# A two-layer decoder step on one core: where the memory block's residual comes from, where the last norm stands, and where staged operands lie

## The chip, the cores and the metric

The kernel runs on 1 core of a Trainium2 chip. The metric is device time in microseconds (us) of the whole program. Engines are named as in the profile: PE (TensorE), DVE (VectorE), ACT (ScalarE), POOL (GpSimd), SP (SyncE, which here only issues DMAs).

## The reference, cut to what matters

One inference step of two layers for a prompt (1 x 1024 tokens) and a sample group (8 x 8 tokens), together 1088 tokens of 1024 features, in float32. Each layer is a mixing block, then cross-attention into 256 memory tokens, then a convolutional feed-forward block:

```python
for l in range(DEPTH):
    ...                                   # l = 0: mix_ab, l = 1: sliding-window attention
    xp = xp + yp
    xs = xs + ys
    ...
    xp = xp + mem_attend(rmsnorm(xp, ln_mem[l]), mk, mv, m_w_q[l], m_q_gain[l], m_w_o[l])
    ...
    fp, cp = conv_ffn(rmsnorm(xp, ln_ffn[l]), zc, f_w_up[l], f_conv_w[l], f_conv_b[l], f_w_down[l])
    ...
    xp = xp + fp

def conv_ffn(h, g_ctx, w_up, conv_w, conv_b, w_down):
    up = h @ w_up
    g, u = up[..., :D_FF], up[..., D_FF:]
    ...                                   # gc = causal conv of g, 3 taps
    y = (gelu(gc) * u) @ w_down
```

## The kernel before

Activations are kept feature-major: 8 blocks of 128 features by tokens. Tokens come in three chunks `CHS` of 384, 384 and 320 (c = 0, 1, 2) for the attention blocks and in two halves of 544 (q = 0, 1) for the feed-forward block. Each float32 operand is split into a high part and a rest (ACT copies to float32r, DVE subtracts), and each product is three matmuls (`mm3`).

PE's order is the program's, written out by hand. The order on the other engines and DMA queues is made by a planner that simulates the program ahead of time; each engine and each queue then runs in order.

**State.** The SBUF tile `big` holds the split residual `xh`, `xl` of all chunks. In feed-forward the same bytes hold `B0`, the operands of half q = 0 in seven products (names 1, 5, 6, 2, 3, 7, 4, in steps of 8 QT with QT = 272 columns); the last 8 QT serve for raw loads (`hx_of`) and for parts to be stored (`part`).

**x_update (L309)** adds a block of output projection to the residual. In the mixing blocks it reads xh and xl, stores the sum to DRAM (`xd`, one tensor for each chunk) and splits it again. In mem() it loads the block from `xd` into a tile of the ring `tmp` (5 buffers), adds on DVE, and stores to `xq`, a DRAM tensor for each half. `squares` (L296) adds the squares into `acc[c]`: block 0 by ACT alone, odd blocks on POOL, even ones on DVE.

**Norms.** `norm_chunk(c)` (L343) takes column sums of `acc[c]` by matmul with ones (L336), then a power on POOL (L331); `factors(c)` (L733) calls `spread`, which puts the factors on a diagonal (DVE, L375), spreads them by matmul (L376) and copies them to `rvq` (L379).

**Output projection of mem()** (L957 on): six jobs (hf, c) in the order (0,0), (1,0), (0,1), (1,1), (0,2), (1,2), each with four blocks m of 12 matmuls. `next(parts)` steps through the attention of the samples in between. The norm of chunk 0 stands ahead of (1,1), that of chunk 1 ahead of (0,2), followed by `build()`, which makes B0; the norm of chunk 2 stands after (1,2).

**ffn() (L1112).** `up_operands` (L1073) loads a raw pair of blocks from `xq` by SP, scales it by gain and factor (L1080) and makes the seven operands (L1092 splits, L1097 differences). Half 1 (tile set `b`) is built before the jobs. Each job of `seven` (L998) is seven products of 12 matmuls; products 7 and 4 of a job run within the next one. `gate_out` and `up_out` empty PSUM; `up_out` stores the operands of the down projection to DRAM (`hd`).

**Down projection** (L1305 on): `load_b` (L1316) loads operands on POOL's queue: 1, 5, 6 come already split, straight into one of 15 rotating tiles (10 of them in `big`); 2, 3, 7, 4 come whole into `hx`, one of 4 pool tiles, and are split by ACT and DVE (L1326, L1327). `down_out` adds `xq` through a tile `xr`.

## Time and profile before

| | |
|---|---|
| Runs | 2695.42, 2697.85, 2699.47 us (median 2697.85) |
| Profiled execution | 2697.89 us, of which its span 2695.8 us |
| PE busy in the span | 93% |
| DVE, ACT, POOL busy | 73%, 45%, 18% |
| Mean granted clock of PE | 0.962 of 2.4 GHz |

A row of a timeline is one instruction or several merged ones: start, duration (for merged ones first to last), engine, line, operation, output and inputs with their shapes, count, and in brackets the time the engine was idle before it and what ended that. The windows give the busy time of each engine within a stretch.

### The profile page before, as it was taken

What the parts mean: (1) busy time and instruction counts of PE and PEld (TensorE: products, weight loads), DVE (VectorE), ACT (ScalarE), POOL (GpSimd) and SP (SyncE); (2) the same over time, 40 slices, a digit from 0 to 9 for tenths busy, and PEclk for the clock granted to TensorE, in tenths of its full rate; (3) what the DMA queues carried; (4) which work ended last, traced back from release to release, by engine and by line L of the source; (5) the groups of instructions that cost most, each with busy time, mean ns of one, the idle gap of its engine ahead of it and who ended that gap; (6) DMA issues with size and microseconds to landing.
All of it is one profiled execution on the core that took longest, in us unless ns stands there. A gap on an engine that the chain in (4) does not pass through costs nothing.

```text
span 2695.8 us, 46361 instructions
## 1 busy us (share of the span) xinstructions
PE 2510.7 (93%) x17136; PEld 2317.7 (86%) x17136; DVE 1962.6 (73%) x4514; ACT 1226.4 (45%) x2687; POOL 481.6 (18%) x440
## 2 busy tenths in 40 slices
PE   8999999769999998999899989998599999998998
PEld 6898987569999998999776767876499999998998
DVE  8646964588777786888657676853888778776885
ACT  5223644254545454433546554552454545544231
POOL 3506432110000001111533333421100000002100
PEclk9999999779999999999999998998799999999999
DMA  8302213534233336553211022215424233347642
GB/s 270 107 19 81 83 57 109 169 97 131 91 129 111 125 123 206 207 197 137 66 38 47 1 69 75 87 45 179 135 89 131 94 126 119 117 153 261 221 136 87
DMA packets 239714, 318.12 MB, mean 118 GB/s; under 512 B 18946, under 2 KB 199264, under 8 KB 239487
## 3 DMA queue, kind: packets, MB, share of 16 engines
q1 hardware_dynamic: 227454, 253.87, 29.4%
q0 software_dynamic: 12032, 61.28, 6.2%
q8 instruction: 135, 2.21, 0.3%
q14 instruction: 93, 0.75, 0.1%
HBM read 224.08 MB, written 90.93 MB: 117 GB/s over the span
## 4 chain that ended last, share of the span: by engine, by line
PE 68%; DVE 12%; issue 7%; DMA 5%; POOL 3%; ACT 2%; SPq 0%; POOLq 0%; DVEq 0%; ACTq 0%
PE psa L1007 8%; PE psa L1009 8%; PE psa L1008 8%; PE psb L1009 6%; PE psb L1007 6%; PE psb L1008 6%; PE psa L259 5%; PE psa L260 5%; PE psa L261 5%; DVE s L350 3%; PE psb L167 2%; DMA hx<-hd 1%; DMA t<-xd 1%; PE psb L842 1%; PE psb L817 1%
## 5 line engine op out<-in xcount | busy, mean ns | idle before, releaser
L1055 ACT ACTIVATE w<-st 128x512 fp32r<-128x512 f32 (+2 forms) x532 | 298.7, 572 | 382.7 <-PE psb L1009 115.3
L1056 DVE TENSOR_TENSOR w<-st,w 128x512 fp32r<-128x512 f32 (+2 forms) x532 | 327.4, 621 | 168.7 <-ACT w L1055 163.1
L1007 PE MATMUL psa<-big,w 128*128 128x272 f32 x1160 | 340.8, 294 | 11.0 <-DVE x L1343 7.3
L1009 PE MATMUL psa<-big,w 128*128 128x272 f32 x1160 | 338.7, 292 | 0.0
L1008 PE MATMUL psa<-big,w 128*128 128x272 f32 x1160 | 337.3, 291 | 0.0
L1007 PE MATMUL psb<-big,w 128*128 128x272 f32 x952 | 276.1, 290 | 19.1 <-ACT big L1326 19.1
L1007 PE MATMUL psa<-b,w 128*128 128x272 f32 x952 | 276.8, 291 | 12.4 <-ACT b L1091 7.0
L1008 PE MATMUL psa<-b,w 128*128 128x272 f32 x952 | 275.8, 290 | 4.4 <-DVE b L1092 4.4
L1009 PE MATMUL psa<-b,w 128*128 128x272 f32 x952 | 276.4, 290 | 0.0
L1009 PE MATMUL psb<-big,w 128*128 128x272 f32 x952 | 276.3, 290 | 0.0
L1008 PE MATMUL psb<-big,w 128*128 128x272 f32 x952 | 275.7, 290 | 0.5 <-DVE big L1327 0.5
L1007 PEld LDWEIGHTS psa<-big,w 128*128 128x128 f32 x1160 | 222.3, 192 | 14.9 <-DVE x L1343 8.7
L1008 PEld LDWEIGHTS psa<-big,w 128*128 128x128 f32 x1160 | 222.3, 192 | 0.0
L1009 PEld LDWEIGHTS psa<-big,w 128*128 128x128 f32 x1160 | 222.1, 191 | 0.0
L260 PE MATMUL psa<-s,w 128*128 128x384 f32 (+1 forms) x576 | 198.4, 344 | 17.9 <-DVE s L350 17.6
L259 PE MATMUL psa<-s,w 128*128 128x384 f32 (+1 forms) x576 | 198.1, 344 | 7.1 <-DVE t L319 3.6
L1322 POOL DMA_DIRECT2D big<-hd x36 | 21.7, 603 | 1022.1 <-PE psa L1009 988.4
L1007 PEld LDWEIGHTS psb<-big,w 128*128 128x128 f32 x952 | 180.9, 190 | 19.6 <-ACT big L1326 19.6
L261 PE MATMUL psa<-s,w 128*128 128x384 f32 (+1 forms) x576 | 194.0, 337 | 0.0
L1007 PEld LDWEIGHTS psa<-b,w 128*128 128x128 f32 x952 | 179.7, 189 | 14.0 <-ACT b L1091 7.4
L1008 PEld LDWEIGHTS psa<-b,w 128*128 128x128 f32 x952 | 180.6, 190 | 5.5 <-DVE b L1092 5.5
L1009 PE MATMUL psb<-b,w 128*128 128x272 f32 x632 | 183.5, 290 | 0.0
(352 smaller groups left out, 6765.6 us busy)
## 6 DMA issues: line engine op xcount, KB each, us to landing
st<-in_f_w_up_dram SPq DMA_DIRECT2D x88, 512.0 KB
hd<-big SPq DMA_DIRECT2D x264, 136.0 KB
hd<-m SPq DMA_DIRECT2D x176, 136.0 KB
hx<-hd POOLq DMA_DIRECT2D x48, 408.0 KB, 6.4
big<-hd POOLq DMA_DIRECT2D x24, 816.0 KB, 7.4
st<-in_f_w_down_dram SPq DMA_DIRECT2D x48, 384.0 KB
b<-hd POOLq DMA_DIRECT2D x12, 816.0 KB, 6.7
big<-xq SPq DMA_DIRECT2D x32, 272.0 KB
```

Source lines behind the costliest of these rows:

```text
L167: T.transpose(out, in_, idt[:rows, :rows])
L259: mm(out, lhsT=ah, rhs=bh, start=first, stop=False)
L260: mm(out, lhsT=ah, rhs=bl, start=False, stop=False)
L261: mm(out, lhsT=al, rhs=bh, start=False, stop=last)
L350: V.tensor_tensor(out=t[:, 1, :src_n], in0=src, in1=f(t[:, 0, :src_n]), op=ALU.subtract)
L817: mm(ps[:, j, :], lhsT=qt[:, 2 * hh + j, :], rhs=kt[:, 2 * hh + j, :], start=True, stop=True)
L842: mm(ps[:, :n], lhsT=vm[:, kb, 128 * h:128 * h + 128], rhs=pts[c][h][:, kb, :n], start=(kb == 0), stop=(kb == 1))
L1007: mm(ps[:, :QT], lhsT=wt[:, 0, k, :], rhs=bt[:, 0, k, :], start=first and k == 0, stop=False, skip_group_check=True)
L1008: mm(ps[:, :QT], lhsT=wt[:, 0, k, :], rhs=bt[:, 1, k, :], start=False, stop=False, skip_group_check=True)
L1009: mm(ps[:, :QT], lhsT=wt[:, 1, k, :], rhs=bt[:, 0, k, :], start=False, stop=k == nk_of(j) - 1, skip_group_check=True)
L1055: S.activation(t[:, 0], src, AF.Copy)
L1056: V.tensor_tensor(out=t[:, 1], in0=src, in1=f(t[:, 0]), op=ALU.subtract)
```

## The change

For chunks 0 and 1 the residual in mem() is added from xh and xl in SBUF; for chunk 2 it is loaded from DRAM, for all eight blocks ahead of the job. Only chunk 2 is therefore stored to `xd`. The norm of chunk 0 moves next to that of chunk 1; the norm of chunk 2 moves into the first up job (column sums after product 5, spread and the operands of half 1 after product 6), and its raw loads go by POOL. In mem() even blocks' squares are added on POOL and odd ones on DVE. In the down projection the four staging tiles `hx` and one `xr` tile move into `big`; 7 of the 15 rotating tiles lie there then, and 8 in the pool.

```diff
+    def squares(c, m, src, place=None, odd=1):
...
-            E = P if m % 2 else V
+            E = P if m % 2 == odd else V
...
-        if xq is None:
-            V.tensor_tensor(out=t1, in0=ps[:, :n], in1=f(xh[c][:, m, :]), op=ALU.add)
-            P.tensor_tensor(out=t1, in0=t1, in1=f(xl[c][:, m, :]), op=ALU.add)
-            nc.sync.dma_start(out=xd[c][:, m, :], in_=t1)
-            split_x(c, m, t1)
-            return
-        nc.sync.dma_start(out=t1, in_=xd[c][:, m, :])
-        V.tensor_tensor(out=t1, in0=ps[:, :n], in1=t1, op=ALU.add)
-        squares(c, m, t1)
+        if c == 2:
+            nc.sync.dma_start(out=xd[:, m, :], in_=t1)
+        split_x(c, m, t1)
+
+    def x_out(c, m, ps, xq, old, place):
+        o, n = CHS[c]
+        t1 = tmp()[:, :n]
+        V.tensor_tensor(out=t1, in0=ps[:, :n], in1=old[0], op=ALU.add)
+        if len(old) > 1:
+            V.tensor_tensor(out=t1, in0=t1, in1=old[1], op=ALU.add)
+        squares(c, m, t1, place, 0)
...
     def norm_chunk(c):
-        for t in range(3 * c, 3 * c + 3):
-            xr[t] = norm_tm(t, f"r{t}")
+        ps = psB()
+        for i in range(3):
+            t = 3 * c + i
+            xr[t] = norm_tm(t, f"r{t}", ps[:, 2 * i:2 * i + 2])
...
-                if j == 3:
-                    norm_chunk(0)
-                    factors(0)
                 if j == 4:
-                    next(parts)
-                    next(parts)
-                    norm_chunk(1)
-                    factors(1)
+                    for _ in range(4):
+                        next(parts)
+                    for i in range(2):
+                        norm_chunk(i)
+                        factors(i)
                     build()
...
                     sp = [split_act(s3p, n, otf[:, k, o:o + n]) for k in range(4)]
+                    if c == 2:
+                        old = []
+                        for i in range(4):
+                            rd = f(s3p.tile([128, 2, 384], F32R, tag="s3", name="rd"))[:, :, :n]
+                            nc.sync.dma_start(out=rd, in_=xd[:, 2 * i:2 * i + 2, :])
+                            old += [rd[:, 0], rd[:, 1]]
...
-                    x_update(c, m, ps, xq)
+                    x_out(c, m, ps, xq, [old[m]] if c == 2 else [f(xh[c][:, m, :]), f(xl[c][:, m, :])], rvq[:, o:o + n] if c == 2 else None)
...
-            norm_chunk(2)
-            factors(2)
-        return xq, rvq, gtail, B0
+        return xq, rvq, gtail, B0, factors
...
-            nc.sync.dma_start(out=raw[:, kh], in_=xq[q][:, 4 * kh + j:4 * kh + j + 1, :])
+            (P if q else nc.sync).dma_start(out=raw[:, kh], in_=xq[q][:, 4 * kh + j:4 * kh + j + 1, :])
...
+            def second_half():
+                factors(2, mtile)
+                with pool(f"fe{l}") as ep:
+                    for j in range(4):
+                        up_operands(l, 1, j, xq, rvq, B[1], ep)
+                gep.append(es.enter_context(pool(f"fge{l}")))
+
+            def begin(out):
+                def first_out(what, ps):
+                    out(what, ps)
+                    if what == "m5":
+                        norm_chunk(2)
+                    elif what == "u2":
+                        second_half()
+                return first_out
...
-                if i < 10:
-                    return region(i * 2 * 3 * QT, 2, 3, QT)
-                return bq.tile([128, 2, 3, QT], F32R, tag="b", name="b", bufs=5)
+                if i < 7:
+                    return region(i * 6 * QT, 2, 3, QT)
+                return bq.tile([128, 2, 3, QT], F32R, tag="b", name="b", bufs=8)
+
+            def htile():
+                staged[0] += 1
+                return f(region(42 * QT + staged[0] % 4 * 3 * QT, 3, QT))
...
-                        hx = ep.tile([128, 3, QT], F32, tag="hx", name="hx", bufs=4)[:, :nk]
+                        hx = htile()[:, :nk]
...
-                    xr = ep.tile([128, 2, HT], F32, tag="xr", name="xr", bufs=2)
+                    xr = ep.tile([128, 2, HT], F32, tag="xr", name="xr") if q else f(region(BIG - 2 * HT, 2, HT))
```

## Rows read from the trace of the kernel before

**Rows 1.** The page: busy time of PE, and its busy tenths in 40 slices.

```profile
PE 2510.7 (93%) x17136; PEld 2317.7 (86%) x17136; DVE 1962.6 (73%) x4514; ACT 1226.4 (45%) x2687; POOL 481.6 (18%) x440
...
PE   8999999769999998999899989998599999998998
```

**Rows 2.** Timeline of PE, layer 0, end of mem() and first up jobs.

```profile
481.62 0.72 PE L336 MATMUL psb<-ones,acc 128*128 128x2 f32 x6
492.14 1.62 PE L376 MATMUL psb<-t,ones 128*128 128x128 f32 x6 [9.79 <-DVE t L375]
...
515.74 0.83 PE L336 MATMUL psb<-ones,acc 128*128 128x2 f32 x6
519.18 1.43 PE L376 MATMUL psb<-t,ones 128*128 128x128 f32 x6 [2.61 <-DVE t L375]
...
567.39 1.32 PE L336 MATMUL psb<-ones,acc 128*128 128x2 f32 x6 [15.91 <-POOL acc L305]
...
588.43 0.59 PE L1008 MATMUL psa<-b,w 128*128 128x272 f32 x1 [0.36 <-DVE b L1092]
```

**Rows 3.** Timeline of DVE in the same stretch.

```profile
491.25 0.56 DVE L319 TENSOR_TENSOR t<-psa,t 128x384 f32<-128x384 f32 x1 [2.47 <-DMA t<-xd]
491.72 0.67 DVE L375 TENSOR_SCALAR t<-idt,r 128x128 f32<-128x128 f32 x3
...
520.65 0.56 DVE L379 COPY rvq<-psb 128x384 f32<-128x384 f32 x1 [0.58 <-PE psb L376]
...
565.35 0.49 DVE L319 TENSOR_TENSOR t<-psa,t 128x320 f32<-128x320 f32 x1 [2.03 <-DMA t<-xd]
...
571.14 0.49 DVE L379 COPY rvq<-psb 128x320 f32<-128x320 f32 x1 [1.04 <-PE psb L376]
```

**Rows 4.** Windows: stretch, length, busy PE, PEld, DVE, ACT, POOL; PEclk, DMA share, GB/s.

```profile
481.60:521.20 39.60, 26.79 (x157) 20.56 (x155) 16.37 (x40) 8.17 (x16) 7.35 (x10) 0.86 0.62 203
521.20:588.40 67.20, 36.80 (x195) 31.18 (x195) 57.51 (x137) 29.91 (x73) 8.51 (x7) 0.70 0.35 108
555.00:571.60 16.60, 3.65 (x14) 3.24 (x15) 7.21 (x20) 2.67 (x5) 3.29 (x5) 0.50 0.49 149
571.60:588.40 16.80, 11.35 (x70) 10.60 (x68) 16.62 (x45) 9.36 (x25) 0.00 (x0) 0.80 0.21 67
...
1060.00:1070.00 10.00, 8.50 (x41) 7.49 (x42) 6.18 (x11) 5.61 (x11) 3.67 (x7) 0.66 0.79 262
1852.90:1892.80 39.90, 27.36 (x157) 20.66 (x155) 16.31 (x40) 8.07 (x16) 7.38 (x10) 0.83 0.64 206
1892.80:1959.00 66.20, 35.97 (x195) 30.43 (x195) 57.40 (x137) 29.95 (x73) 8.51 (x7) 0.73 0.35 107
```

**Rows 5.** Timeline of POOL: two adds of squares, and one DMA issue.

```profile
541.95 3.46 POOL L305 TENSOR_TENSOR acc<-acc,t 128x320 f32<-128x320 f32 x1 [22.21 <-ACT t L303]
...
559.49 0.86 POOL L305 TENSOR_TENSOR acc<-acc,t 128x320 f32<-128x320 f32 x1 [7.71 <-ACT t L303]
...
1037.82 0.73 POOL L1322 DMA_DIRECT2D big<-hd  x1 [8.10 <-PE psa L1009]
```

**Rows 6.** Windows as in rows 4: a stretch of layer 0's first output projection.

```profile
322.00:332.00 10.00, 10.00 (x62) 10.00 (x61) 10.00 (x17) 9.27 (x20) 3.55 (x4) 1.00 0.16 57
```

**Rows 7.** Timelines of PE, POOL and SP at the start of layer 0's down projection.

```profile
1061.20 0.59 PE L1007 MATMUL psb<-big,w 128*128 128x272 f32 x1 [9.84 <-ACT big L1326]
...
1053.86 0.72 POOL L1322 DMA_DIRECT2D big<-hd  x1 [10.78 <-DMA hd<-big]
1054.58 2.18 POOL L1325 DMA_DIRECT2D hx<-hd  x4
...
1051.64 0.39 SPq L1225 DMA_DIRECT2D hd<-m  x1
```

**Rows 8.** The page's DMA issues: count, size of each, us from issue to landing.

```profile
big<-hd POOLq DMA_DIRECT2D x24, 816.0 KB, 7.4
```

**Rows 9.** Timeline of SP in the stretch of rows 2.

```profile
552.36 0.38 SPq L1047 DMA_DIRECT2D st<-in_f_w_up_dram  x1
```

More of the change, by code (lines that the diff above doesn't have):

```diff
@@ L285, with new_acc @@
     acc = [None] * 3
-    def new_acc(c):
-        acc[c] = R["tmp"].tile([128, CHS[c][1]], F32, tag=f"acc{c}", name=f"acc{c}")
+    def new_acc(c, place):
+        acc[c] = R["tmp"].tile([128, CHS[c][1]], F32, tag=f"acc{c}", name=f"acc{c}") if place is None else place
     def split_x(c, m, src, alt=False):
@@ L294, in split_x @@
         squares(c, m, src)
-    def squares(c, m, src):
+    def squares(c, m, src, place=None, odd=1):
         n = CHS[c][1]
         if m == 0:
-            new_acc(c)
+            new_acc(c, place)
             S.activation(acc[c], src, AF.Square)
@@ L303, in squares, with x_update @@
             S.activation(sq[:, :n], src, AF.Square)
-            E = P if m % 2 else V
+            E = P if m % 2 == odd else V
             E.tensor_tensor(out=acc[c], in0=acc[c], in1=sq[:, :n], op=ALU.add)
-    xd = [dp.tile([128, KB, n], F32, name=f"xd{c}") for c, (_, n) in enumerate(CHS)]
-    def x_update(c, m, ps, xq=None):
+    xd = dp.tile([128, KB, CHS[2][1]], F32, name="xd")
+    def x_update(c, m, ps):
         n = CHS[c][1]
         t1 = tmp()[:, :n]
-        if xq is None:
-            V.tensor_tensor(out=t1, in0=ps[:, :n], in1=f(xh[c][:, m, :]), op=ALU.add)
-            P.tensor_tensor(out=t1, in0=t1, in1=f(xl[c][:, m, :]), op=ALU.add)
-            nc.sync.dma_start(out=xd[c][:, m, :], in_=t1)
-            split_x(c, m, t1)
-            return
-        nc.sync.dma_start(out=t1, in_=xd[c][:, m, :])
-        V.tensor_tensor(out=t1, in0=ps[:, :n], in1=t1, op=ALU.add)
-        squares(c, m, t1)
-        o = CHS[c][0]
+        V.tensor_tensor(out=t1, in0=ps[:, :n], in1=f(xh[c][:, m, :]), op=ALU.add)
+        P.tensor_tensor(out=t1, in0=t1, in1=f(xl[c][:, m, :]), op=ALU.add)
+        if c == 2:
[8 more added lines that the diff above has]
+        squares(c, m, t1, place, 0)
         for q in range(2):
@@ L331, in rsq, with norm_tm @@
         P.tensor_tensor(out=out, in0=ms[:in_.shape[0], :w], in1=mhalf[:in_.shape[0], :w], op=ALU.pow)
-    def norm_tm(t, tag="r"):
+    def norm_tm(t, tag="r", ps=None):
         c, o, w = tile_of(t)
-        ps = psB()
+        ps = psB() if ps is None else ps
         mm(ps[:w, 0:2], lhsT=acc[c][:, o:o + w], rhs=ones[:, 0:2], start=True, stop=True)
@@ L373, in spread @@
             _, o, w = tile_of(t)
-            dg = tmp()[:, 0:128] if pl is None else pl.tile([128, 128], F32, tag="dg", name="dg", bufs=3)
+            dg = pl()[:, 0:128] if callable(pl) else pl.tile([128, 128], F32, tag="dg", name="dg", bufs=3)
             V.tensor_scalar(dg[:w, :w], idt[:w, :w], rs[t][:w], None, op0=ALU.mult)
@@ L731, in mem, with factors @@
         B0 = {i: region(2 * 4 * QT * n, 2, 4, QT) for n, i in enumerate("1562374")}
-        def factors(c):
+        def factors(c, pl=tmp):
             o, n = CHS[c]
-            spread(c, xr, None, rvq[:, o:o + n])
+            spread(c, xr, pl, rvq[:, o:o + n])
         with ExitStack() as es:
@@ L1109, in combos_b, with ffn @@
         split("4", comb(x21, t2, x21))
-    def ffn(l, xq, rvq, gtail, B0, rs):
+    def ffn(l, xq, rvq, gtail, B0, factors, rs):
         PARTS = "156"
@@ L1133, in ffn @@
             R["tc"] = 2
-            with pool(f"fe{l}") as ep:
-                for j in range(4):
-                    up_operands(l, 1, j, xq, rvq, B[1], ep)
-            gep = es.enter_context(pool(f"fge{l}"))
             ges = {}
+            gep = []
+            def second_half():
[12 more added lines that the diff above has]
+                return first_out
             halo = {}
@@ L1280, in jobs @@
                         for q in range(2):
-                            yield w, B[q], outs(pair, q)
+                            out = outs(pair, q)
+                            yield w, B[q], out if pair or up or q else begin(out)
             for _ in seven(jobs()):
```

3 lines of the change are left out of this document (2 added, 1 removed).

## The prediction

> **What bounds the kernel now.** I read the busy shares first, then PE's (TensorE's) waits in order of time, then the load of DVE (VectorE) between those waits. PE is busy for 93% of the span, and its slices dip in four places [rows 1]: at the end of each mem() with the start of ffn(), and at each start of the down projection. Only these holes are for sale.
>
> In PE's timeline of layer 0 [rows 2] the reader is to see three holes. At 481.62, after the last matmul of the output projection's job (0,1), PE runs the first norm's column sums, and that norm's spread comes only at 492.14, 9.79 us idle. After job (1,2) PE waits 15.91 us until POOL has added the last squares, at 567.39. Then the first up job runs; the second gets under way at 588.43.
>
> Why: DVE waits for the residual, tile after tile, from DRAM [rows 3]. The last residual add (565.35) waited 2.03 us for `t<-xd`; the one at 491.25 waited 2.47, and the diagonals of the first norm (491.72) stand right behind it in DVE's order. So the first hole is not the norm's own length: where nothing holds it up, the same chain takes from 515.74 to 519.18, 3.4 us [rows 2].
>
> The windows [rows 4] give DVE's load. Between 481.6 and 521.2 it works 16.37 of 39.6 us. From 521.2, where the copy that begins at 520.65 [rows 3] has the factors of chunks 0 and 1 ready, to 588.4 it works 57.51 of 67.2, and the idle 9.7 us lie nearly all between 555.0 and 571.6 (7.21 of 16.6 busy). **From 521 on DVE sets the pace**: operand building fills 571.6 to 588.4 (16.62 of 16.8). Layer 1 repeats it: 16.31 of 39.9, then 57.40 of 66.2.
>
> **Part 1: residual from SBUF, first norm later.** For chunks 0 and 1 the DRAM load goes and one DVE add of 0.56 us [rows 3] comes, 16 in a layer, 9 us. They lie before 521.2, where DVE has 23 us free: cost nothing; without that cover up to 9 us. With the first norm moved, PE goes from (0,1) at 481.6 straight to (1,1). What follows took from 493.4 (the spread's six matmuls end) to 515.7, 22.3 us. The clock of 0.86 in that window says that part of it ran at the lower of two levels; for the restart after the hole I take off 1.7 us, an estimate between 0 and 4. So the samples' scores end at 481.6 + 20.6 = 502.2. Then two norms stand in a row. One, from column sums to the spread's end, is 515.74 to 520.5, 4.7 us; the other ends with the factors' copy at 521.2, 5.5 us. Factors are ready at 502.2 + 4.7 + 5.5 = 512.4, **8.8 us earlier**. In layer 1, whose windows begin at the same two points, 1852.9 and 1892.8, the way is 0.3 us longer and I take 9.2. The two additional `next(parts)` reach empty yields only and move nothing.
>
> **Part 2: chunk 2 and the last norm.** Chunk 2's residual is loaded into tiles that (1,1) frees, some 25 us before its first use, by four loads on SP where there were eight. Its DVE adds stay (0.49). Of the squares DVE adds four instead of three, +0.5 us, and the chain ends without POOL. The last norm now stands inside the first up job: PE runs three products before it has to spread, and DVE can fill its idle time with weight splits. What it can't fill is part of the norm's own chain, 567.39 to the copy at 571.14 [rows 2, 3], 3.8 us. I leave DVE 2 us of idle time (bounds 0, all filled, and 9.7, nothing filled). DVE's way to the second up job is then 57.5 + 0.5 + 2 = 60 us where it was 67.2: **7.2 us**. Layer 1: 59.9 against 66.2, **6.3 us**. The transitions gain 16.0 and 15.5, together 31.5. Cross-check by PE: the first half's operands are done some 34 us after the factors (521.2 to 555.0, DVE busy throughout), so at 546.5; with three products and the norm's chain the last factors are there at 554; 16.8 us of operands and 1.5 of weights later it is 572, against 588.4. Bounds for a layer: 9 (Part 1 alone works) and 19 (no idle time and earlier weights).
>
> Eight raw loads of the second half go from SP's queue to POOL's, past its adds for chunk 2 and the last norm's powers, which stand behind a load that waits for a store or a buffer; for the powers wait DVE's diagonals and PE's spread. At 0.73 us an issue [rows 5] that is 5.8 us, in a stretch where POOL has little else: zero, and the far bound is rival (a). For that bound: POOL's add of squares took 3.46 us at 541.95, where DVE was full, and 0.86 at 559.49, where it was not [rows 5]; four times. The Trainium skill (SBUF — State Buffer, § SBUF: two separate sides) says that VectorE and GpSimd take a shared port pair as an exclusive lock, and warns that a DMA issued from GpSimd starves while its descriptors can't be written; it would have these loads left on SP. The add's row agrees with a lock; no row here shows issues under a full DVE.
>
> Sixteen of 24 residual stores go from SP in each output projection ahead of mem(), where DVE is full (10.00 of 10 [rows 6]): zero, bounds 2 us either way. The three norms' sums in one PSUM tile and the `xr` tiles (two before, two after) cost nothing.
>
> **Part 3: down projection.** PE waits 9.84 us at 1061.20 for a split of `hx`, whose loads go only at 1054.58, behind a POOL load that waited 10.78 us for a store [rows 7]. The restart runs at 0.66 of the clock (1060 to 1070 [rows 4]), 3.4 us more. With `hx` in the shared region, under B0's operands 7 and 4, its loads can go when these are last read, from 1037.8 (the load that waits for just this now [rows 5]), and land some 7 us later [rows 8]: the first down job has no hole and ends near 1054.3. What is late next: the second half's direct loads, which now need pool tiles that lie where the up stage's outputs were. The last of those is stored at 1051.64; a store of that moment had landed by 1053.86 [rows 7]. So they go at 1054 and land near 1060. Job two now starts near 1065, two products after 1061.20. I take **4 us a layer**, 8 in all; bounds 9 (tiles free at 1050) and -2 (the loads share the queue and land at 1067).
>
> **Sum.** 31.5 + 8 = 39.5. The profiled execution took 2697.89 us (span 2695.8 and 2.1 around it), the median is 2697.85: one base. 2697.9 - 39.5 = 2658; I take 2660, since each hole was costed at a good order of the queues.
>
> **Rivals.** (a) POOL's queue: issues stretched fourfold as the add was, 2.9 us each. Four of them, 12 us, follow chunk 2's stores at about 544 and take 6 us to land: 562, where the factors are ready at 554; 9 us late a layer, 2660 + 18 = **2678**. For: DVE is full there. Against: an issue isn't an add. [...] (b) DVE's order puts the last norm's steps behind other work and none of the 7 us is won: 2697.9 - 18 = **2680**. (c) Slower: chunk 2's residual loads stand on SP's in-order queue behind the weight load that goes at 552.36 [rows 9]. At 7.4 us for 816 KB [rows 8] their 1.3 MB land at 563; with four of eight groups in PSUM the adds end at 571, the factors come at 577, the second up job at 594 instead of 588.4: +5.6 a layer, **2709**, without a gain at the down start. It decides once they land later than about 557. Against: they are emitted before that weight load. (d) It doesn't do what it says, the holes only change place: **2694 to 2700**. (e) Better: DVE without idle time and pool tiles free at 1050: **2645**.
>
> **How the numbers follow.** Forecast 0.62 (its own range 2650 to 2672), (e) 0.08, (a) 0.13, (b) 0.07, (d) 0.04, (c) 0.06. The bounds (9 to 19 a transition, -2 to 9 a down start) give gains of 14 to 56; all four at one end is unlikely, so 2642 to 2684, which holds (a), (b) and (e). About 0.2%, 5.4 us, can be told from no change: faster 0.62 + 0.08 + 0.13 + 0.07 = 0.90, same 0.04, slower 0.06.
>
> **What would show it.** Right: PE without a wait over 5 us between (0,1) and the scores; DVE nowhere waiting for `xd`, and some 60 us from the factors of chunks 0 and 1 to the second up job; in the first down job no wait for an `hx` split, in the second one for a direct load. Wrong: second-half operands waiting for raw loads on POOL (a); DVE idle ahead of the last factors (b); DVE waiting for a residual load (c). If the two norms in a row cost PE over 10 us, Part 1 is mis-sized.

## The result and the profile after

| | runs, us | median, us | ratio to before, 95% interval |
|---|---|---|---|
| before | 2692.88 to 2699.47 (4) | 2696.64 | |
| after | 2673.42 to 2676.40 (4) | 2674.50 | 0.9920, 0.9902 to 0.9937 |

The change gains 22 us of the 38 that were forecast. The kernel before ran again beside the later experiments, with medians of 2692.71, 2693.53 and 2693.37; by those the gain is 18 to 19. The ratios of the experiments are to those runs. The profiled execution took 2676.40 us, its span is 2674.6, 21.2 less than before. To see where they went I cut the span at five points of PE's order that every kernel here has. These rows of PE's timeline are the cuts in the kernel after (the second cut is that DVE wait of the second up job which answers to 587.02 before; the third is the first wait for `pT` behind the feed-forward block):

```profile
457.69 1.91 PE L884 MATMUL psb<-k,qm 128*32 128x256 f32 x8
...
575.41 0.60 PE L1017 MATMUL psa<-b,w 128*128 128x272 f32 x1 [1.74 <-DVE b L1101]
...
1321.82 0.66 PE L167 MATMUL psb<-idt,pT 128*128 128x128 f32 x2 [6.24 <-DVE pT L1488]
...
1825.57 1.70 PE L884 MATMUL psb<-k,qm 128*32 128x256 f32 x7
...
1940.93 0.59 PE L1017 MATMUL psa<-b,w 128*128 128x272 f32 x1 [1.73 <-DVE b L1101]
```

So there are five stages: **T0** from the samples' first scores to the second up job (the transition of layer 0, with the output projection), **F0** the rest of layer 0's feed-forward up to the next block's first products, **M** the sliding-window attention and what follows up to layer 1's scores, **T1**, and **F1** to the end. In us, one profiled execution each; all kernels of the experiments below are in the table already. The runs of one kernel lie 2.5 to 15 us apart, so a row is not a median: e3's profiled execution is its fastest run, the one of the change its slowest.

| kernel | ahead of T0 | T0 | F0 | M | T1 | F1 | span |
|---|---|---|---|---|---|---|---|
| before | 456.9 | 130.1 | 738.7 | 502.5 | 129.4 | 738.2 | 2695.8 |
| after | 457.7 | 117.7 | 746.4 | 503.8 | 115.4 | 733.7 | 2674.6 |
| e1_no_down | 456.9 | 116.5 | 739.8 | 501.9 | 116.6 | 732.5 | 2664.2 |
| e2_down_only | 453.9 | 129.3 | 745.1 | 501.7 | 128.9 | 735.6 | 2694.6 |
| e3_last_norm_out | 454.2 | 116.0 | 742.6 | 497.6 | 115.2 | 731.3 | 2656.9 |
| e4_raw_on_sp | 456.8 | 117.5 | 744.3 | 505.6 | 116.4 | 732.6 | 2673.2 |
| e5_both_back | 456.2 | 115.1 | 740.4 | 503.9 | 116.4 | 731.4 | 2663.3 |
| e6_residual_only | 457.1 | 119.8 | 741.6 | 504.1 | 119.7 | 733.3 | 2675.5 |
| e7_sum_tiles | 457.5 | 114.1 | 743.1 | 502.1 | 114.0 | 734.5 | 2665.4 |
| e8_sums_first | 456.9 | 113.9 | 741.7 | 499.7 | 115.1 | 728.9 | 2656.2 |
| e9_sums_down_back | 457.4 | 114.4 | 741.1 | 502.7 | 114.7 | 733.2 | 2663.4 |
| e10_sums_last_out | 455.4 | 115.3 | 745.0 | 503.1 | 113.6 | 731.2 | 2663.7 |
| e11_sums_norm0_back | 456.0 | 117.7 | 744.3 | 501.1 | 116.8 | 733.7 | 2669.5 |

After against before: the transitions gave 12.4 and 14.0, together 26.4 (forecast 31.5). F0 lost 7.7 and F1 gained 4.5, so the feed-forward blocks together lost 3.2 (forecast a gain of 8). M lost 1.3 and the start 0.8. The sum is 21.1. The two transitions together repeat well where the code in them is the same: 233.1, 233.1 and 233.9 us (after, e1, e4), 231.2 and 231.5 (e3, e5), 229.0 and 229.1 (e8, e9).

**The transition.** PE's timeline of layer 0 after the change, against [rows 2]:

```profile
503.15 1.91 PE L884 MATMUL psb<-k,qm 128*32 128x256 f32 x8 [1.77 <-ACT k L876]
...
506.68 0.38 PE L341 MATMUL psb<-ones,acc 128*128 128x2 f32 x2 [1.30 <-DVE s L335]
507.31 0.38 PE L341 MATMUL psb<-ones,acc 128*128 128x2 f32 x2 [0.25 <-DVE s L335]
...
550.99 0.56 PE L341 MATMUL psb<-ones,rvq 128*128 128x2 f32 x2 [4.82 <-DVE rvq L305]
...
554.25 0.37 PE L341 MATMUL psb<-ones,rvq 128*64 128x2 f32 x2 [1.87 <-DVE s L335]
...
558.04 1.81 PE L383 MATMUL psb<-m,ones 128*128 128x128 f32 x6 [0.40 <-DVE m L382]
...
573.08 0.59 PE L1016 MATMUL psa<-b,w 128*128 128x272 f32 x1 [6.75 <-ACT b L1100]
```

The holes of 9.79 and 15.91 us are gone; the longest waits left are the 4.82 us for the last squares and the 6.75 us in the second up job. New is the pattern `ones,... [.. <-DVE s L335]`: a norm's three column sums lie in one PSUM tile, and each sum waits until DVE has read (L335) the one ahead of it. DVE's timeline shows why the last of them took so long:

```profile
550.36 0.48 DVE L305 TENSOR_TENSOR rvq<-rvq,t 128x320 f32<-128x320 f32 x1
...
551.58 0.16 DVE L335 TENSOR_SCALAR s<-psb 128x1 f32<-128x1 f32 x1 [0.28 <-PE psb L341]
553.44 0.69 DVE L1065 TENSOR_TENSOR w<-st,w 128x512 fp32r<-128x512 f32 x1 [1.70 <-ACT w L1064]
554.04 0.15 DVE L335 TENSOR_SCALAR s<-psb 128x1 f32<-128x1 f32 x1
...
559.89 0.49 DVE L386 COPY rvq<-psb 128x320 f32<-128x320 f32 x1 [1.65 <-PE psb L383]
```

Between the first and the second read stands a weight split (L1065) that waits 1.70 us for ACT. From the last squares (550.84) to the factors (560.38) it is 9.5 us. Before, the same way was 567.39 to 571.63, 4.2 [rows 2, 3].

Windows (columns as in [rows 4]), from the factors of chunks 0 and 1 to the second up job, in either layer:

```profile
514.75:576.82 62.07, 38.18 (x196) 32.24 (x196) 57.63 (x137) 29.91 (x73) 10.41 (x14) 0.72 0.37 114
1880.92:1942.35 61.43, 36.18 (x196) 30.50 (x196) 57.64 (x137) 30.02 (x73) 10.25 (x14) 0.72 0.36 115
```

DVE's work was forecast at 58.0 us and is 57.6; its idle time was taken as 2 us and is 4.4 and 3.8.

**The down projection's start**, layer 0. PE from the up stage's last wait to the second down job, the later waits of the stage, and what DVE, POOL, SP and ACT did:

```profile
1037.13 0.59 PE L1016 MATMUL psa<-b,w 128*128 128x272 f32 x1 [2.66 <-DVE m L1287]
...
1049.24 0.60 PE L1016 MATMUL psa<-b,w 128*128 128x272 f32 x1 [5.03 <-DMA b<-hd]
...
1066.39 0.39 PE L1016 MATMUL psa<-b,w 128*128 128x272 f32 x1 [1.87 <-ACT x L1373]
...
1295.38 0.60 PE L1016 MATMUL psa<-b,w 128*128 128x272 f32 x1 [4.21 <-DVE x L1375]
...
1034.55 0.73 DVE L1359 TENSOR_TENSOR big<-big 128x544 fp32r<-128x544 f32 x1 [1.00 <-ACT big L1358]
...
1051.88 0.57 POOL L1354 DMA_DIRECT2D b<-hd  x1 [6.64 <-DMA hd<-big]
...
1045.03 0.42 SPq L1366 DMA_DIRECT2D xr<-xq  x1
1052.82 0.32 SPq L1366 DMA_DIRECT2D big<-xq  x1
1057.07 0.91 SPq L1056 DMA_DIRECT2D st<-in_f_w_down_dram  x2
...
1064.27 0.42 ACT L1064 ACTIVATE w<-st 128x256 fp32r<-128x256 f32 x1 [3.83 <-DMA st<-in_f_w_down_dram]
```

The wait for the `hx` split (9.84 us, [rows 7]) is gone. The second job waits 5.03 us for its direct loads. PE's order behind the second up job is the same in all kernels here, so the same matmuls can be compared. The first window is the kernel after, from a matmul ahead of the up stage's last wait to one in the down jobs; the second is the same stretch of the kernel before:

```profile
1031.78:1106.89 75.11, 62.91 (x443) 61.03 (x442) 47.41 (x110) 34.01 (x79) 13.49 (x25) 0.91 0.71 250
```

```profile
1043.80:1116.90 73.10, 60.65 (x443) 58.04 (x442) 47.32 (x108) 35.23 (x81) 14.71 (x27) 0.93 0.72 252
```

Up to the second down job it takes 17.5 us where it took 21.2, a gain of 3.7, near the 4 forecast (3.5 in layer 1). The 379 matmuls behind that take 5.7 longer, so the place loses 2.0 us in all (1.4 in layer 1). One cause lies ahead of the down projection. The `hx` loads go earlier, as forecast, and with them the work that they set off: among the outputs of the last up job DVE also splits an `hx` tile, for which it waits 1.00 us for ACT (1034.55). PE's wait for those outputs is 2.66 us at 1037.13, and was 0.83 at the same matmul before:

```profile
1047.31 0.39 PE L1007 MATMUL psa<-b,w 128*128 128x272 f32 x1 [0.83 <-DVE m L1262]
```

From the first matmul of that window to the one behind this wait it takes 4.6 to 5.8 us in layer 0 of all seven kernels with the new tiles and 3.7 in the six with the old. All waits of PE over 0.1 us in the window sum to 12.2 us after and 12.4 before: the one hole has become several smaller waits.

The rest of F0's 7.7 us lies further on: 4.4 at and behind the last down job, and 1.4 at a wait in the middle (1156.00). e1 and e2 ask what of it belongs to this part of the change. Of the 4.5 us that F1 gained, 3.7 lie at the same place in the middle, where PE had waited 5.46 us for DVE before (2540.55) and waits 2.18 now (2520.87); no part of the prediction names it.

### The profile page after: what moved, and what is told of

It reads as the page before. It is cut to its first block, busy times and chain, and to the rows that moved or that the text cites. A ratio compares the mean times of both kernels' runs of the same rounds, so it can differ in the third digit from the quotient of the medians.

```text
span 2674.6 us, 46246 instructions
## 1 busy us (share of the span) xinstructions
PE 2517.4 (94%) x17136; PEld 2324.2 (87%) x17136; DVE 1983.9 (74%) x4552; ACT 1227.9 (46%) x2687; POOL 480.3 (18%) x450
## 5 line engine op out<-in xcount | busy, mean ns | idle before, releaser
L1065 DVE TENSOR_TENSOR w<-st,w 128x512 fp32r<-128x512 f32 (+2 forms) x532 | 326.2, 618 | 179.0 <-ACT w L1064 171.8
L1016 PE MATMUL psa<-b,w 128*128 128x272 f32 x1056 | 310.0, 294 | 41.3 <-ACT b L1100 12.9
L1017 PE MATMUL psa<-b,w 128*128 128x272 f32 x1056 | 308.3, 292 | 7.4 <-DVE b L1101 7.4
L1016 PE MATMUL psa<-big,w 128*128 128x272 f32 x1056 | 310.3, 294 | 4.2 <-DVE x L1375 2.0
L1018 PE MATMUL psa<-big,w 128*128 128x272 f32 x1056 | 309.4, 293 | 0.0
L1018 PE MATMUL psa<-b,w 128*128 128x272 f32 x1056 | 308.8, 292 | 0.0
L1017 PE MATMUL psa<-big,w 128*128 128x272 f32 x1056 | 307.9, 292 | 0.0
L1016 PEld LDWEIGHTS psa<-b,w 128*128 128x128 f32 x1056 | 201.4, 191 | 44.8 <-ACT b L1100 13.4
L1016 PE MATMUL psb<-b,w 128*128 128x272 f32 x792 | 230.6, 291 | 0.0
L1018 PE MATMUL psb<-b,w 128*128 128x272 f32 x792 | 230.5, 291 | 0.0
L1018 PE MATMUL psb<-big,w 128*128 128x272 f32 x792 | 229.5, 290 | 0.3 <-DVE w L1065 0.3
L1017 PE MATMUL psb<-b,w 128*128 128x272 f32 x792 | 229.8, 290 | 0.0
L1016 PE MATMUL psb<-big,w 128*128 128x272 f32 x792 | 229.1, 289 | 0.0
L1017 PE MATMUL psb<-big,w 128*128 128x272 f32 x792 | 228.3, 288 | 0.0
L260 PE MATMUL psa<-s,w 128*128 128x384 f32 (+1 forms) x576 | 197.2, 342 | 14.2 <-DVE s L357 13.8
L1017 PEld LDWEIGHTS psa<-b,w 128*128 128x128 f32 x1056 | 202.2, 191 | 9.4 <-DVE b L1101 9.4
L1016 PEld LDWEIGHTS psa<-big,w 128*128 128x128 f32 x1056 | 203.3, 193 | 6.2 <-DVE x L1375 2.6
L1017 PEld LDWEIGHTS psa<-big,w 128*128 128x128 f32 x1056 | 203.3, 192 | 0.0
L1018 PEld LDWEIGHTS psa<-big,w 128*128 128x128 f32 x1056 | 203.0, 192 | 0.0
L1018 PEld LDWEIGHTS psa<-b,w 128*128 128x128 f32 x1056 | 201.8, 191 | 0.0
L259 PE MATMUL psa<-s,w 128*128 128x384 f32 (+1 forms) x576 | 196.8, 342 | 5.1 <-ACT s L356 5.1
```

The lines of the kernel that those rows point to most:

```text
L259: mm(out, lhsT=ah, rhs=bh, start=first, stop=False)
L260: mm(out, lhsT=ah, rhs=bl, start=False, stop=False)
L1016: mm(ps[:, :QT], lhsT=wt[:, 0, k, :], rhs=bt[:, 0, k, :], start=first and k == 0, stop=False, skip_group_check=True)
L1017: mm(ps[:, :QT], lhsT=wt[:, 0, k, :], rhs=bt[:, 1, k, :], start=False, stop=False, skip_group_check=True)
L1018: mm(ps[:, :QT], lhsT=wt[:, 1, k, :], rhs=bt[:, 0, k, :], start=False, stop=k == nk_of(j) - 1, skip_group_check=True)
L1065: V.tensor_tensor(out=t[:, 1], in0=src, in1=f(t[:, 0]), op=ALU.subtract)
```

## The experiments

The theory from these rows: the transition gained what DVE allowed, and the down projection's new places gave nothing. Rivals: the raw loads on POOL's queue are what is missing; or the last norm's move is.

**e1_no_down** is the change with the down projection's tiles as before:

```diff
-                if i < 7:
-                    return region(i * 6 * QT, 2, 3, QT)
-                return bq.tile([128, 2, 3, QT], F32R, tag="b", name="b", bufs=8)
+                if i < 10:
+                    return region(i * 2 * 3 * QT, 2, 3, QT)
+                return bq.tile([128, 2, 3, QT], F32R, tag="b", name="b", bufs=5)
...
-                        hx = htile()[:, :nk]
+                        hx = ep.tile([128, 3, QT], F32, tag="hx", name="hx", bufs=4)[:, :nk]
...
-                    xr = ep.tile([128, 2, HT], F32, tag="xr", name="xr") if q else f(region(BIG - 2 * HT, 2, HT))
+                    xr = ep.tile([128, 2, HT], F32, tag="xr", name="xr", bufs=2)
```

> The changed kernel with the down projection as it was: 10 of 15 operand tiles in the shared region, hx and xr in the pool. Theory: the 22 us come from the two ends of mem(), 11 and 14 us by the trace of the changed kernel, and the down part is worth nothing in layer 0 (it moves the hole to the second half's operands and the next weights). Then this takes 2671 to 2677 us, and the hole of some 10 us at the first hx split is back at both down starts. Rival: the down part is worth the 8 us forecast and the ends of mem() only 14; then 2681 to 2685.

Measured: 2666.39 us (2662.54 to 2676.09), ratio 0.9901 (0.9877 to 0.9926), below both ranges. It is 8 us under the change by the medians, but its interval overlaps that of e4 (0.9913 to 0.9945), whose time is the change's, so the 8 us are not clear of the noise.

**e2_down_only** is the kernel before with that part alone (the same edit the other way).

> The kernel before with nothing but the down part: 7 of 15 operand tiles in the shared region, the four staging tiles and one xr tile there too. Theory: within 3 us of the kernel before (2694 to 2700), with the 10 us wait for an hx split gone and in its place a wait of some 5 us for a direct load of the second half and waits of ACT and DVE for the next down weights. Rival: 8 us faster, 2687 to 2690.

Measured: 2697.52 us (2691.53 to 2703.19), ratio 1.0015 (1.0005 to 1.0026), as the theory has it.

What follows: the part gains nothing by itself; put on the kernel before it costs 4 us. The profiled execution shows the cost in F0, 745.1 in e2 and 738.7 without; there the other stages are shorter by as much (F1 by 2.6, the start by 3.0), which this part doesn't explain. Besides the up stage's end above, two places repeat. Behind the last down job, from its wait to the first wait for `pT`, it takes 26.2 to 26.5 us in all seven kernels with the new tiles (1295.38 to 1321.82 above) and 23.3 to 23.5 in the six with the old ones; and that wait itself is 4.2 us with the new tiles and 2.9 with the old. e1's PE timeline:

```profile
1289.90 0.40 PE L1016 MATMUL psa<-b,w 128*128 128x272 f32 x1 [2.88 <-DVE x L1369]
...
1313.18 0.66 PE L167 MATMUL psb<-idt,pT 128*128 128x128 f32 x2 [4.36 <-DVE pT L1482]
```

ACT's timelines show the difference. With the old tiles (e1) the copies for the next block's second chunk begin 1.3 us ahead of the last job, and the eviction of the convolution's tail follows later:

```profile
1288.57 1.10 ACT L1403 ACTIVATE t<-x 128x160 f32<-128x160 f32 x4
...
1292.29 0.49 ACT L1320 ACTIVATE st<-psb 110x384 f32<-110x384 f32 x1
```

With the new ones (after) the eviction, which needs PE's work of the last job, comes first, and the copies stand behind it:

```profile
1298.73 0.49 ACT L1320 ACTIVATE st<-psb 110x384 f32<-110x384 f32 x1 [3.68 <-PE psb L167]
...
1300.31 0.60 ACT L1409 ACTIVATE t<-x 128x160 f32<-128x160 f32 x2
```

That is so in all thirteen kernels, 4.7 to 4.9 us behind the last job's start with the new tiles and 1.3 us ahead of it with the old. One more thing goes with it, in a row of SP's waits (line and releaser; total, times, longest) of the kernel after for 1240 to 1295:

```profile
SPq L1467 <- PE psa L1018: 13.6, 1, 13.6
```

L1467 and the lines behind it load the next block's gains and tables. Their tiles wait for PE's matmuls of the down projection. That fits the pool's 5 operand tiles having become 8, so that the next block's tiles lie under one that is read late; where the tiles lie isn't shown. With the old tiles these loads go some 16 us ahead of the last job and not 4. Whether this wait made the planner order ACT as it did, or the tiles otherwise, wasn't tried.

The second place is the start. The `xr` tile in `big` waits until the stores to `hd` have left its bytes: `big<-xq` goes at 1052.82, 7.3 us after the queue was ready, and the next weight loads stand behind it on SP (1057.07). ACT waits 3.83 us for them at 1064.27 with PSUM's evictions behind it, and PE waits 1.87 for those at 1066.39.

**e3_last_norm_out** moves the last norm and the second half's operands back ahead of the up jobs:

```diff
+            norm_chunk(2)
+            factors(2)
         return xq, rvq, gtail, B0, factors
...
-                factors(2, mtile)
                 with pool(f"fe{l}") as ep:
...
-            def begin(out):
-                def first_out(what, ps):
-                    out(what, ps)
-                    if what == "m5":
-                        norm_chunk(2)
-                    elif what == "u2":
-                        second_half()
-                return first_out
+            second_half()
...
-                            yield w, B[q], out if pair or up or q else begin(out)
+                            yield w, B[q], out
```

> The changed kernel with the last norm and the second half's operands back ahead of the up jobs; residual, first norm and down part as changed. Theory: DVE sets the pace, so where PE meets the last norm matters little: the norm's chain is 4.3 us there instead of 9.4, but DVE finds no weight work during it; 2672 to 2678. Rival: standing inside the first up job is what hides the chain; then this loses most of the first job's time, 5 to 7 us a layer, 2684 to 2688.

Measured: 2662.16 us (2658.68 to 2666.05), ratio 0.9885 (0.9864 to 0.9905). Both expectations missed: it is 12 us faster than the change by the medians, and 17.7 by the profiled executions. The transitions gain only 1.7 and 0.2 us of that. PE waits longer for the norm, at 546.50 and 550.59, and less in the second up job:

```profile
546.50 0.56 PE L341 MATMUL psb<-ones,rvq 128*128 128x2 f32 x2 [7.91 <-DVE rvq L305]
...
550.59 0.38 PE L341 MATMUL psb<-ones,rvq 128*64 128x2 f32 x2 [2.69 <-DVE s L335]
...
567.85 0.39 PE L1018 MATMUL psa<-b,w 128*128 128x272 f32 x1 [3.88 <-ACT b L1102]
```

Where the last norm stands is nearly indifferent, since DVE sets the pace on either side of it. The rest came in stages that the edit does not touch: M 6.2, F0 3.8, F1 2.4, and 3.5 ahead of T0.

**e4_raw_on_sp** puts the second half's raw loads back on SP:

```diff
-            (P if q else nc.sync).dma_start(out=raw[:, kh], in_=...)
+            nc.sync.dma_start(out=raw[:, kh], in_=...)
```

> The changed kernel with the second half's raw loads on SP's queue instead of POOL's. Theory: no difference, 2672 to 2677, since the eight issues take 0.54 to 0.74 us each in the trace of the changed kernel, the first four before the last factors are ready. Rival: POOL's issues hold the last norm's powers or the operands up; then 3 to 8 us faster, 2666 to 2671.

Measured: 2675.82 us (2672.94 to 2676.90), ratio 0.9929 (0.9913 to 0.9945): no difference from the change. POOL's timeline of the kernel after says why, with DVE busy for the whole window around it:

```profile
536.00:550.00 14.00, 10.17 (x73) 9.95 (x71) 14.00 (x30) 8.26 (x19) 5.39 (x6) 0.97 0.49 145
```

```profile
537.74 0.54 POOL L1086 DMA_DIRECT2D big<-xq  x1 [3.66 <-DVE big L1101]
538.31 1.81 POOL L305 TENSOR_TENSOR rvq<-rvq,t 128x320 f32<-128x320 f32 x1
543.52 0.94 POOL L305 TENSOR_TENSOR rvq<-rvq,t 128x320 f32<-128x320 f32 x1 [3.40 <-DVE rvq L305]
544.75 0.55 POOL L1086 DMA_DIRECT2D big<-xq  x1 [0.29 <-DMA xq<-t]
```

Beside an equally full DVE one add of POOL took 1.81 us and another 0.94; the two issues took no longer than one at 1051.88 above (0.57), where DVE is not full.

The next four kernels ask whether e1's and e3's gains add, what the move of the first norm is worth, and what the shared PSUM tile costs. **e5_both_back** is e1's edit and e3's together.

> The change with two parts undone: the last norm and the second half's operands ahead of the up jobs, and the down projection's tiles as before; kept are the residual from SBUF, the first norm moved behind job (1,1) and the raw loads on POOL. Theory, the two costs are separate (one in the transition, one in the down projection and in the loads behind it): 2674.5 less 8 less 12, 2652 to 2658, no direct-load wait in the second down job, and the wait ahead of the next layer's first transposes back from 6.2 to 4.4 us. Rival, both gains are the same shift of the later stages and don't add: 2660 to 2666.

Measured: 2666.23 us (2661.45 to 2673.80), ratio 0.9897 (0.9869 to 0.9925). The gains don't add; the rival is right, at the edge of its range. T0 and T1 (115.1, 116.4) keep what e3 had. M is back at 503.9.

**e6_residual_only** has in addition the first norm back ahead of job (1,1) and the raw loads on SP; the residual's source is what is left:

```diff
+                if j == 3:
+                    norm_chunk(0)
+                    factors(0)
                 if j == 4:
-                    for _ in range(4):
-                        next(parts)
-                    for i in range(2):
-                        norm_chunk(i)
-                        factors(i)
+                    next(parts)
+                    next(parts)
+                    norm_chunk(1)
+                    factors(1)
```

> As e5_both_back, but the first norm stands ahead of job (1,1) again and the raw loads are on SP: of the change only the residual's source is left (with the squares' accumulation that goes with it). Theory, the hole of 9.8 us was DVE's wait for the residual, so it shrinks to the norm's own 3 us or so without the norm being moved, and the later pair of norms is one norm shorter: 2652 to 2662, within 4 us of e5_both_back. Rival, the move of the first norm is what gives the gain: the hole stays at 8 to 10 us and the time is 2668 to 2675.

Measured: 2676.23 us (2666.14 to 2681.15), ratio 0.9923 (0.9897 to 0.9949). The time is just above the rival's, the mechanism is the theory's. The hole is not 8 to 10 us: the norm's chain runs from 482 to 486.2 with waits of 0.6 us at most, so it was the residual from DRAM that had made the 9.8 us. Yet each transition is 4.7 and 3.3 us longer than in e5. PE's timeline shows what the norm still costs there:

```profile
482.67 0.38 PE L341 MATMUL psb<-ones,acc 128*128 128x2 f32 x2 [0.60 <-DVE s L335]
...
485.78 0.80 PE L383 MATMUL psb<-t,ones 128*128 128x128 f32 x2 [0.50 <-DVE t L382]
...
487.01 0.52 PE L261 MATMUL psa<-s,w 128*128 128x384 f32 x1
```

4.4 us of small matmuls and waits, and behind them matmuls of 0.52 us that took 0.33 ahead of it: the 12 us around it have a granted clock of 0.86, those of e5 in the same place 1.00. So of the 26.4 us the residual's source gave 20.0 (259.5 to 239.5 for both transitions), with what e6 keeps beside it: the early loads for chunk 2, the squares' order and the shared PSUM tile, which were not tried apart. The first norm's move gave 8.0 (to 231.5; the raw loads' queue, which differs too, is worth 0.8 in e4); the last norm's move took 1.6 back (to 233.1 in e1 and after).

**e7_sum_tiles** is e5 with a PSUM tile for each column sum:

```diff
     def norm_chunk(c):
-        ps = psB()
         for i in range(3):
             t = 3 * c + i
-            xr[t] = norm_tm(t, f"r{t}", ps[:, 2 * i:2 * i + 2])
+            xr[t] = norm_tm(t, f"r{t}")
```

> As e5_both_back, but each of a norm's three column sums has a PSUM tile of its own, as in the kernel before. Theory, in one tile each sum waits until DVE has read the one ahead of it, and DVE reads in its order behind weight splits: with tiles of their own the waits of 2 to 3 us ahead of the third sum go, 1 to 3 us a layer, 2 to 6 us less than e5_both_back. Rival, the reads stand behind the same weight split in DVE's order whichever tile they read: within 1.5 us of e5_both_back.

Measured: 2665.44 us (2663.33 to 2669.23), ratio 0.9893 (0.9869 to 0.9917), by the total the rival's. By the transitions it is the theory's: 1.0 and 2.4 us less than e5, which the feed-forward stages give back (F0 and F1 are 5.8 longer). A total alone can't tell the two here.

**e8_sums_first** is the change with the one tile kept, but the three sums issued ahead of the three reads:

```diff
         for i in range(3):
+            _, o, w = tile_of(3 * c + i)
+            mm(ps[:w, 2 * i:2 * i + 2], lhsT=acc[c][:, o:o + w], rhs=ones[:, 0:2], start=True, stop=True)
+        for i in range(3):
             t = 3 * c + i
-            xr[t] = norm_tm(t, f"r{t}", ps[:, 2 * i:2 * i + 2])
+            w = tile_of(t)[2]
+            r = xr[t] = small(f"r{t}", 1, 1)
+            rsq(r[:w], ps[:w, 2 * i:2 * i + 1], 1.0 / D)
```

> The change, with the three column sums of a norm issued one behind the other and the reads behind all three, in the same one PSUM tile. Theory, the sum that waits 1.9 us for DVE's read and what follows from it go: 2668 to 2673. Rival, DVE's order (its weight splits wait for ACT, the diagonals stand behind them) sets the time of the last factors, not the sums: 2673 to 2676.

Measured: 2658.08 us (2657.57 to 2660.06), ratio 0.9866 (0.9839 to 0.9893): 16 us faster than the change, below both ranges, and the fastest kernel of the study. The sums now run as one group, `x6`, and the reads as one, `x3`:

```profile
548.77 1.29 PE L352 MATMUL psb<-ones,rvq 128*128 128x2 f32 x6 [4.67 <-DVE rvq L305]
```

```profile
550.09 0.28 DVE L335 TENSOR_SCALAR s<-psb 128x1 f32<-128x1 f32 x3 [1.01 <-PE psb L352]
...
554.84 0.48 DVE L391 COPY rvq<-psb 128x320 f32<-128x320 f32 x1
```

From the last squares (548.62) to the factors (555.32) it is 6.7 us where the change needs 9.5. The transitions gain 3.8 and 0.3, 4.1 together; e9 against e1, the same edit with the old tiles, gives 4.0. That is all that the edit itself can claim, and of layer 0's 3.8 some 0.9 is a shorter wait of the samples' scores for ACT ahead of the first sums (0.88 us, 1.77 in the kernel after). M gains 4.1, F0 4.7, F1 4.8.

**A stage far from the edit.** M is 497.6 and 499.7 in e3 and e8 and 501.1 to 505.6 in all others. PE's order there is the same in all thirteen kernels, and one stretch sets the two apart: the 112 matmuls from the samples' last scores into the output projection, in layer 1's sliding-window attention, take 20.1 and 20.3 us in e3 and e8, and 25.1 to 27.9 in the other eleven. The rest of M, 474.8 to 479.4, doesn't set the two apart. The windows show it in the kernel after and in e8:

```profile
1583.13:1608.99 25.86, 20.24 (x126) 18.60 (x117) 21.17 (x33) 15.00 (x41) 9.29 (x5) 0.87 0.31 86
```

```profile
1573.73:1594.00 20.27, 17.85 (x126) 16.37 (x117) 17.76 (x27) 15.13 (x41) 8.80 (x5) 1.00 0.23 67
```

The other engines' order is the planner's, made for the whole program, and in these two kernels it differs just there: SP issues 13 loads of the output weights in a row, then the samples' cached values, then the other 3; in the change it issues 15 and 1. In the kernel after, ACT's weight split stands ahead of the splits that PE needs and waits for such a load:

```profile
1586.80 1.06 ACT L233 ACTIVATE w<-st 128x1024 fp32r<-128x1024 f32 x1 [2.84 <-DMA st<-in_c_w_o_dram]
...
1590.78 0.44 PE L260 MATMUL psa<-s,w 128*128 128x384 f32 x1 [1.66 <-DVE s L357]
```

In e8 the split has moved behind one more of those, and doesn't wait:

```profile
1576.10 1.06 ACT L233 ACTIVATE w<-st 128x1024 fp32r<-128x1024 f32 x1
...
1580.12 0.45 PE L260 MATMUL psa<-s,w 128*128 128x384 f32 x1 [0.40 <-DVE s L362]
```

In e3 the split has moved in the same way but still waits 2.05 us for its load. So the two share both orders, the loads' and the splits', and the runs don't tell which of them counts. PE's waits in the stretch sum to 2.6 and 2.4 us in e3 and e8 and to 4.6 to 5.9 in the others; the rest of the difference goes with the granted clock, 0.87 in the first of the windows and 1.00 in the second.

So the theory became: add up the stages, not the totals. A kernel's T and F come from its edits, and M from the order of these loads, which can be read from the program before it runs. The last three kernels, each e8 with one part put back, test it against the plain addition of gains.

**e9_sums_down_back** is e8 with the down part of e1's diff.

> e8_sums_first with the down projection's tiles as before. Theory, from the stages of the runs so far: the transitions stay at e8's (114 and 115 us from the first scores to the second up job), the first layer's feed-forward gains some 3 us by the old tiles, but the loads of the second mixing block's output weights stand in SP's order as in the change (15 in a row, where e8_sums_first has 13 and then the samples' cache), so that block loses the 4 us that e8 had gained there: 2660 to 2667. Rival, the parts' gains add (16 of e8, 8 of e1): 2648 to 2654.

Measured: 2664.65 us (2662.58 to 2665.29), ratio 0.9886 (0.9869 to 0.9902).

**e10_sums_last_out** is e8 with the diff of e3.

> e8_sums_first with the last norm and the second half's operands ahead of the up jobs. Theory, where the last norm stands is worth less than 2 us in a transition either way, and the output weights' loads stand in the change's order again: transitions 114 to 116 us each, the mixing block between them 4 us longer than in e8, 2660 to 2667. Rival, the norm inside the job costs what e3 showed (12 us) and this adds to e8's gain: 2644 to 2650.

Measured: 2666.31 us (2665.60 to 2669.77), ratio 0.9897 (0.9882 to 0.9912).

**e11_sums_norm0_back** is e8 with the first norm back, as in e6's diff.

> e8_sums_first with the first norm ahead of job (1,1) again. Theory, PE and DVE lose there what e6_residual_only lost against e5_both_back, 4 us a transition (118 to 120 us each), and the output weights' loads stand in the change's order: 2667 to 2676. Rival, with the residual in SBUF the norm's place is indifferent and only the loads' order counts: 2660 to 2664.

Measured: 2672.73 us (2671.24 to 2677.00), ratio 0.9921 (0.9906 to 0.9936).

All three totals lie in the theory's ranges and outside the rivals'. The transitions are 229.1 in e9 and 228.9 in e10, where e8 has 229.0, so with the sums first the last norm's place is worth nothing at all. In e11 they are 234.5, 5.5 us more for the first norm's place. M is 501.1 to 503.1, 1.4 to 3.4 us above e8's 499.7 where 4 was forecast; the stretch above is 25.1 to 27.0 us, as in the other kernels with 15 loads in a row. Two more forecasts of stages were off: F0 in e9 (741.1) is only 0.6 below e8's 741.7 where some 3 were expected, and e11's transitions are 117.7 and 116.8 where 118 to 120 was expected.

**What stays open.** F0 and F1 scatter among kernels whose code there is the same: 741.7 to 746.4 and 728.9 to 733.7 with the new tiles, down part and change together. Compared by the same matmuls, nearly all of it lies in few places: the 441 matmuls around the down projection's start (70.7 to 75.1 us in layer 0 with the new tiles, 73.1 to 75.3 with the old), one wait in the middle of the down projection, and the first matmuls; the up stage behind those takes 427.0 us in all thirteen kernels. The orders of ACT and DVE differ there by single places, as in M, but I haven't shown for each which place costs what. That some 4.3 us at and behind the last down job of layer 0 go with the new tiles is settled; layer 1 has no such place, since the program ends there. The whole price of the down part isn't: by the totals undoing it gained 8 us on the change (e1) and lost 6.6 on e8 (e9), and adding it cost 4 (e2). By the stages it is on average +3.4 in F0 (744.2 over seven kernels against 740.8 over six) and -1.4 in F1. That M's gain comes from the planner's order in the stretch rests on the trace and on the thirteen kernels; an edit that moves those loads or splits alone wasn't run.

## Why the prediction was right in sign and put the gain 16 us too high

**What bounds the kernel: right.** The holes were DVE's wait for the residual, and DVE set the pace from the factors on. e6 shows it: the residual's source, with what goes with it, gives 20 us with no norm moved.

**Part 1: right in layer 1, 1.5 us too large in layer 0.** From the first scores to the factors of chunks 0 and 1 it took 64.3 us before and 57.1 after (457.7 to 514.75) in layer 0, a gain of 7.2 where 8.8 was forecast; in layer 1 64.6 and 55.4, 9.2 and 9.2. The term that was too small is the 20.6 us from job (0,1) to the end of the samples' scores. The first sums come 47.3 us after the scores' start in layer 0, where the forecast puts them at 45.3, and the scores themselves wait 1.77 us for ACT at 503.15; in layer 1 they don't, and the sums come at 45.9. The two norms in a row were sized well: 9.8 and 9.5 us from the first sums to the factors, 10.2 forecast, with the waits of the shared PSUM tile (506.68, 507.31) in them. That "the three norms' sums in one PSUM tile" cost nothing failed all the same: with tiles of their own (e7) the pair takes 8.7 and 8.5 us, and the last norm's chain, 9.5 and 8.9 in the kernel after, takes 6.7 and 7.9 with the sums first (e8).

**Part 2: the work was right, the idle time wasn't.** 57.6 us of DVE work against 58.0 forecast; idle 4.4 and 3.8 against 2. With that the gains are 5.1 and 4.8 where 7.2 and 6.3 were forecast. The idle time is in the last norm's chain, 9.5 us with weight splits between its steps, of which one waits for ACT. I had let weight splits fill DVE's idle time; I hadn't asked what they wait for, and that the chain's next step stands behind them. This is rival (b) in part: its mechanism occurred, with some 2 us a layer and not the 7 that it was priced at. That the norm's place inside the first job was the lever was wrong: e3 and e10 have the same transitions without it, within 1.9 us. What made the stretch shorter is in e6 already, with the residual's source and no norm moved: DVE idles 5.3 and 3.5 us there, before the change 9.7 and 8.8.

**Part 3: right up to the second down job, wrong for the stage.** The first down job has no wait for a split, and the second job comes 3.7 and 3.5 us earlier by the same matmuls, against 4 forecast. Over the next 379 matmuls that is lost, and 2.0 and 1.4 more. The sum of 8 us failed because I costed the tiles that moved at their first use only. The earlier loads bring the `hx` splits into the last up job, where DVE makes PE wait. The tiles' later neighbours pay too: the `xr` tile in `big` waits for the last stores with SP's weight loads behind it, and the three additional operand tiles in the pool lie, it seems, where the next block's tiles want to be; with them the next block's copies start 6 us later against the last job. I had written that the `xr` tiles cost nothing. And the restart at the lower clock, which I had let disappear with the hole, stayed: the 10 us behind the wait of 5.03 us have a granted clock of 0.75, and the 10 behind the hole of 9.84 had 0.72 before.

**The rivals.** (a) was wrong: e4 makes no difference, and the issues took 0.54 and 0.55 us beside a DVE without a gap. The Trainium skill (SBUF — State Buffer, § SBUF: two separate sides) says that a DMA issued from GpSimd is starved of descriptors while VectorE runs an operation in a two-port performance mode; an operation with two SBUF inputs takes the lock, by that section, only against a GpSimd operation that reads SBUF. The prediction left that condition out. Beside the eight issues of either layer stood only operations of DVE on two operands, so they are not the case of the warning, and none took over 0.74 us; no run here shows an issue under an operation in such a mode. POOL's own add of 1.81 us agrees with the lock, the one of 0.94 beside as full a DVE doesn't show it. (b)'s price of 2680 leaves Part 3's 8 us out of the gain without saying so; with them it is 2672. (c) didn't occur: DVE waits for `xd` nowhere. (d) is what became of the down projection, and of it alone.

**The sum.** Of the 39.5 us forecast, 5.1 are missing in the transitions and 11.2 in the feed-forward blocks (3.2 lost where 8 was to be gained), and 2.1 went in M and the start: 39.5 - 18.4 = 21.1.

## What to carry to other kernels

Where a planner sets the order of all engines but one, cut the span into stages at fixed instructions of the hand-ordered engine and compare stages; a total mixes the edit with reorderings far from it, which here changed one stretch of 20 us by 5 to 8 us with edits 1000 us away. When a tile moves, cost each byte's earlier and later owner, each queue that stands behind the new wait, and the work that an earlier load sets off on engines that are busy then, not the first use alone. Small results that are read one by one by a busy engine should all be produced ahead of the first read; three sums in a row ahead of their reads were worth up to 4 us in two transitions here. Most of the 16 us by which that kernel is faster comes from elsewhere.

## What the runs showed of the hardware

A DMA issue on POOL was not stretched by a DVE full of two-operand work (0.54 and 0.55 us, at 537.74 and 544.75 above), while an add on POOL in the same stretch took 1.81 us where the next took 0.94. A hole half as long cost nearly the same restart: granted clock 0.75 in the 10 us behind 5.03 us of waiting, 0.72 behind 9.84. And behind 4.4 us of a norm's small matmuls and waits, without a single wait above 0.6 us, the matmuls took 0.52 us each where they had taken 0.33 (e6, from 486.7 to 488.6).
